# State-space stage of a hybrid decoder layer: x's transposes and the spread of a group norm's factor emitted later in the first six groups

## The chip, the cores and the metric

One core of a Trainium2 chip runs the whole kernel. The metric is the time of one execution in device microseconds (us); of several runs the median is told. Engines are named as the profile names them: PE (TensorE, matmuls), DVE (VectorE), ACT (ScalarE), POOL (GpSimd) and SP, whose queue issues the DMAs.

## The reference

One layer over 544 columns: 512 tokens of a prompt and 8 x 4 sample tokens, with 1024 channels. Cut to the part that matters here:

```
z, xbc, dt, q, k, v, qi, ki, wi, g_ssd, g_att = split(u @ w_in)
xbc = silu(causal_dwconv(xbc, buf, conv_w, conv_b))      # width 4
x, B, C = split(xbc)                  # 8 groups: 256 of x, 128 of B, 128 of C each
a_cs = cumsum(dt * a)                 # in chunks of 128 tokens
y_diag = (C @ B^T * decay) @ (x * dt)                    # inside a chunk
state  = B^T @ (x * dt * to_end)                         # from chunk to chunk
y = (y_diag + C @ state * exp(a_cs) + d_skip * x) * silu(z)
y = y * rsqrt(mean(y*y over the 256 channels of a group) + eps) * norm_g
merged = sigmoid(g_ssd) * (y @ w_br_ssd) + sigmoid(g_att) * (y_att @ w_br_att)
```

Before it lies a feed-forward network, after it the projection `w_out`, attention to a memory and a second feed-forward network. The sample tokens' attention `y_att` picks 256 keys of a paged cache by an indexer and gathers their rows. All is fp32.

## The kernel before, in words

Activations lie with channels on the 128 partitions and the 544 columns along the free axis. A product of weights is made in fp32 precision as three passes over operands that are split in a high and a low part (`mm`, line 310: wh·uh, wh·ul, wl·uh, each as 256 and 288 columns, so a product of 8 k-blocks has 48 matmuls). `weights` loads a panel by SP (L267), ACT casts its high part `wh` (L270), DVE subtracts the low part `wl` (L271). `split` does the same for an activation (L318 on ACT, L319 on DVE).

The order of the work is made by `weave` (L104 to L130) when the program is built. Each part of the work is a generator; `yield cost, delay` adds `cost` to a virtual clock and lets that generator sleep for `delay` more. The first generator in the list whose time has come goes on; the last one is the filler. So a `delay` sets how much of other generators' work is emitted before the next step of this one. The engines then run their own queues in the emitted order, and wait by semaphores for one another.

In the state-space stage (`ssd`, L1265) three generators are woven:

- the sample's attention: rounds of the indexer's top k, `sample_select`, `sample_att`. It turns the chosen slots into row addresses, gathers rows `kv` of the cache, transposes the gathered keys (pkT, L1644), makes the scores and the weights `Pm`, turns these (pPT, L1673) and copies them to PN (DVE, L1677), and multiplies by the values (pO, L1681, L1688);
- `tails`: for each of 8 groups g (0 to 7) `ssd_y(g)`: C·B (pcb, L1351; masked to cb by DVE, L1353), B's transposes (pbt, L1357), then after a delay x's transposes (pxt, L1367: four blocks of each of the group's two tiles of x, XO0 and XO1), from which DVE makes xd and xe (L1368, L1370), decay factors abc (ACT, then a product with cb on POOL or DVE, L1380), the sample's small pieces (pcs, L1384; Bs, L1401), chunk states (pst, L1413), the sample's states, y (pY, pYo), and the norm: mean of squares (st, L341), rsqrt in small steps on DVE (L345 to L331), then after a delay the factor's spread over partitions (DVE writes a diagonal zt, L352 and L354; PE spreads it, psr, L355 and L356), y times factor (L1522) and the store to `yssd_d`;
- the filler `fronts`: for each group `ssd_x(g)`, four products of 128 channels in the order B, C, XO0, XO1, each followed by copies (ACT, L1316), four convolution taps (ACT L1324, DVE L1326 three times), tanh (ACT, L1328) and a last DVE step (L1329); then `ssd_z(g)`, two products and their zt. Products of group g+2 start when y of group g is done. After the last group come the load and split of the attention's output (`att_in`, L1712) and eight products with `w_br_att` (`att_out`), times a gate `gt` (L1720).

After the stage the rows of the convolution's state are turned and stored (L1536 to L1539), and `merge` follows: it loads the 16 tiles of y (yt, L1748, three buffers), splits them into yh and yl, woven with what is left of `att_out`, and multiplies them by `w_br_ssd`.

The lines of the change are L1360 (the delay between B's and x's transposes), and L333, L348 and L1518 (the delay between the mean and the spread of the factor; line 1518 is the only caller in this stage).

Of the kernel before, what the change touches and what calls it, by code (L numbers as in the profile page):

```python
# [168 lines left out]
class Net:  # L169
# [160 lines left out]
            nc.vector.tensor_tensor(t, t, xh, op=ALU.mult)  # L330
            nc.vector.scalar_tensor_tensor(y, t, 1.5, y, op0=ALU.add, op1=ALU.mult)  # L331

    def rms(self, sqs, inv_n, pool):  # L333


        nc = self.nc
        st = self.ps1("st")
        blk = [(i * P, min(P, T - i * P)) for i in range(5)]
        for i, (c0, n) in enumerate(blk):
            for j, sq in enumerate(sqs):  # L340
                nc.tensor.matmul(st[:n, i:i + 1], sq[:, c0:c0 + n], self.ones[:, :1], start=(j == 0), stop=(j == len(sqs) - 1))  # L341
        w = pool.tile([P, 4, 5], F32, tag="nw", name="nw", bufs=2)
        x, xh, y, t = (w[:, i, :] for i in range(4))
        nc.vector.memset(x, 1.0)
        nc.vector.tensor_scalar(x[:, :4], st[:, :4], inv_n, EPS, op0=ALU.mult, op1=ALU.add)  # L345
        nc.vector.tensor_scalar(x[:32, 4:], st[:32, 4:5], inv_n, EPS, op0=ALU.mult, op1=ALU.add)
        self.rsqrt(y, x, xh, t)
        yield 0.3, 4.0  # L348

        sq = sqs[0]  # L350
        ps = self.ps1("psr")
        nc.vector.tensor_tensor(sq[:, :TP].rearrange("p (i c) -> p i c", i=4), self.ident.unsqueeze(1).broadcast_to([P, 4, P]),  # L352
                                y[:, :4].unsqueeze(2).broadcast_to([P, 4, P]), op=ALU.mult)
        nc.vector.tensor_scalar(sq[:32, TP:], self.ident[:32, :32], y[:32, 4:], None, op0=ALU.mult)  # L354
        nc.tensor.matmul(ps, self.ones, sq[:, :TP], start=True, stop=True)  # L355
        nc.tensor.matmul(st[:, 64:96], self.ones[:32, :], sq[:32, TP:], start=True, stop=True)  # L356
        yield 1.0
        return ps, st[:, 64:96]
# [979 lines left out]
    def ssd_y(self, g, z):  # L1338
        nc, I, O, sp = self.nc, self.I, self.O, self.sp
# [17 lines left out]
            nc.tensor.transpose(ps[:, c * P:(c + 1) * P], BO[:, c * P:(c + 1) * P], self.ident)  # L1357
        Bt = sp.tile([P, 4, P], F32, tag="hT_", name="Bt", bufs=2)
        nc.scalar.copy(Bt.rearrange("p a b -> p (a b)"), ps)
        yield 0.5, 2.5  # L1360
        hcol = lambda t: t.rearrange("p (c h) -> p c h", c=4)[:, :, 4 * g:4 * g + 4]
        xd = sp.tile([P, 4, 4, 64], F32, tag="xd", name="xd")
        xe = sp.tile([P, 4, 4, 64], F32, tag="xe", name="xe")
# [151 lines left out]
        nc.vector.tensor_tensor(zts[0], zts[0], zts[1], op=ALU.add)  # L1515
        sqs = zts[:1]
        yield 0.0, 9.0
        r, rs = yield from self.rms(sqs, 1.0 / 256, sp)  # L1518
        for i in range(2):
            tl = 2 * g + i  # L1520
            for o, m in ((Y[i][:, :TP], r), (Y[i][:, TP:], rs)):
# [563 lines left out]
```

## Time and profile before

| | |
|---|---|
| time, median of 3 runs | 2201.06 us (2200.52 to 2204.1) |
| the profiled execution | 2201.23 us, span 2199.4 us |
| mean granted clock of PE, profiled | 0.979 |
| PE busy in the span | 2101.4 us (96%) |
| DVE, ACT, POOL busy | 1324.2, 955.2, 444.4 us |
| state-space stage and start of the merge | about 850 to 1450 us |

The times of the trace are microseconds from the start of the span. The span is 1.8 us shorter than the execution's own time, which is 0.17 us over the median. PE is busy nearly all the time; its waits are told by a view of their own, and the granted clock (1.00 is the full one) is told for any stretch.

### The profile page before, as it was taken

The numbers are of one execution on the slowest core, as the hardware profiler recorded it, in microseconds if no ns is written. First come the engines' busy times: TensorE is split into PE (matmuls) and PEld (weight loads), VectorE is DVE, ScalarE is ACT, GpSimd is POOL, SyncE is SP. The second block draws the span as 40 slices with busy tenths as digits, with TensorE's granted clock in tenths as the row PEclk, the third lists the DMA queues.
The fourth block names the chain that finished last, engine by engine and source line by source line (L and its number), as shares of the span: only waits on it lengthen the run. The fifth ranks groups of instructions, "written<-read, shape, count | busy, mean of one in ns | idle before, by whom it ended". The sixth has DMA issues, their size and how long they took to land.

```text
span 2199.4 us, 41232 instructions
## 1 busy us (share of the span) xinstructions
PE 2101.4 (96%) x16675; PEld 1960.6 (89%) x16675; DVE 1324.2 (60%) x2711; ACT 955.2 (43%) x1821; POOL 444.4 (20%) x461
## 2 busy tenths in 40 slices
PE   7999999999999999998999999999999979999998
PEld 7999999998788678897888889999987879999998
DVE  6543334475697989896677668544563475424455
ACT  6323345345445665453556445323535443222233
POOL 0000011032122302225555641012320320000011
PEclk9999999999999999998999999999999999999999
DMA  6424565347442223355456636564443433233243
GB/s 199 126 82 128 165 203 197 113 133 213 135 127 83 88 77 110 117 157 161 126 174 192 178 106 186 175 190 155 144 149 139 154 115 115 76 96 90 81 131 100
DMA packets 320107, 301.70 MB, mean 137 GB/s; under 512 B 25416, under 2 KB 290632, under 8 KB 318868
## 3 DMA queue, kind: packets, MB, share of 16 engines
q1 hardware_dynamic: 310508, 272.58, 40.5%
q0 software_dynamic: 8448, 25.18, 3.7%
q8 instruction: 131, 2.15, 0.4%
q10 hardware_dynamic: 960, 1.31, 0.2%
q14 instruction: 60, 0.49, 0.1%
HBM read 261.14 MB, written 37.35 MB: 136 GB/s over the span
## 4 chain that ended last, share of the span: by engine, by line
PE 72%; DVE 13%; DMA 6%; ACT 4%; issue 3%; POOL 2%; SPq 0%; DVEq 0%; ACTq 0%; POOLq 0%
PE pg L310 42%; PE pgh L310 14%; PE pmo L591 2%; DVE wl L271 2%; ACT wh L270 2%; DMA wr<-in_ffn_wu 1%; DVE gtm L1077 1%; DVE XO L1326 1%; DMA yt<-yssd_d 1%; DMA abc<-ac_d 1%; PE pmkT L1811 1%; POOL sqh L370 1%; PE pmo L1878 1%; DVE XO L1329 1%; DMA wr<-in_ffn_wg 1%
## 5 line engine op out<-in xcount | busy, mean ns | idle before, releaser
L270 ACT CAST wh<-wr 128x1024 fp32r<-128x1024 f32 (+3 forms) x362 | 341.6, 959 | 512.1 <-PE pg L310 288.2
L271 DVE TENSOR_TENSOR wl<-wr,wh 128x1024 fp32r<-128x1024 f32 (+3 forms) x338 | 391.1, 1171 | 222.6 <-ACT wh L270 215.8
L310 PE MATMUL pg<-uh,wh 128*128 128x256 f32 (+1 forms) x2336 | 504.1, 297 | 0.8 <-DVE zt L1291 0.8
L310 PE MATMUL pg<-ul,wh 128*128 128x256 f32 (+1 forms) x2336 | 493.4, 292 | 0.0
L310 PE MATMUL pg<-uh,wl 128*128 128x256 f32 (+1 forms) x2336 | 491.6, 291 | 0.0
L310 PEld LDWEIGHTS pg<-uh,wh 128*128 128x128 f32 x2336 | 380.4, 191 | 21.2 <-issue 17.2
L310 PEld LDWEIGHTS pg<-ul,wh 128*128 128x128 f32 x2336 | 381.2, 191 | 2.9 <-issue 2.2
L310 PEld LDWEIGHTS pg<-uh,wl 128*128 128x128 f32 x2336 | 380.0, 190 | 1.8 <-issue 1.4
L310 PE MATMUL pgh<-uh,wh 128*128 128x288 f32 (+2 forms) x880 | 260.8, 299 | 9.5 <-ACT wh L270 6.1
L310 PE MATMUL pgh<-uh,wl 128*128 128x256 f32 (+2 forms) x880 | 260.3, 298 | 7.3 <-DVE wl L271 7.3
L310 PE MATMUL pgh<-ul,wh 128*128 128x256 f32 (+1 forms) x880 | 257.1, 294 | 0.0
L310 PEld LDWEIGHTS pgh<-uh,wh 128*128 128x128 f32 (+1 forms) x880 | 170.4, 195 | 13.2 <-ACT wh L270 7.0
L310 PEld LDWEIGHTS pgh<-uh,wl 128*128 128x128 f32 (+1 forms) x880 | 169.5, 193 | 11.1 <-DVE wl L271 10.1
L310 PEld LDWEIGHTS pgh<-ul,wh 128*128 128x128 f32 x880 | 171.4, 195 | 0.9 <-issue 0.8
L370 POOL TENSOR_TENSOR sqf<-sqf,sqt 128x256 f32<-128x256 f32 (+1 forms) x48 | 52.4, 1092 | 508.9 <-ACT sqt L369 508.6
L310 PE MATMUL pgh<-hh,wh 128*128 128x288 f32 (+1 forms) x352 | 101.9, 290 | 0.0
L310 PE MATMUL pgh<-hh,wl 128*128 128x288 f32 (+1 forms) x352 | 101.2, 288 | 0.3 <-DVE wl L271 0.3
L310 PE MATMUL pgh<-hl,wh 128*128 128x288 f32 (+1 forms) x352 | 101.4, 288 | 0.0
L1326 DVE SCALAR_TENSOR_TENSOR XO<-CB,convw,XO 128x600 f32<-128x600 f32 x96 | 86.2, 899 | 7.1 <-ACT XO L1324 6.6
L702 POOL DMA_INDIRECT G<-in_cache_kidx,ix x16 | 16.4, 1025 | 361.7 <-DVE ix L697 281.2
L617 DVE TENSOR_TENSOR g<-pg,rt 128x544 f32<-128x544 f32 x32 | 23.2, 725 | 101.1 <-PE pg L310 101.1
L620 DVE TENSOR_TENSOR g<-pg,g 128x544 f32<-128x544 f32 x32 | 23.2, 725 | 99.1 <-PE pg L310 99.1
(608 smaller groups left out, 3875.4 us busy)
## 6 DMA issues: line engine op xcount, KB each, us to landing
wr<-in_w_in SPq DMA_DIRECT2D x66, 512.0 KB
wr<-in_ffn_wg SPq DMA_DIRECT2D x48, 512.0 KB
wr<-in_ffn_wu SPq DMA_DIRECT2D x48, 512.0 KB
wr<-in_ffn_wd SPq DMA_DIRECT2D x44, 384.0 KB
wr<-in_ffn_wd SPq DMA_DIRECT2D x44, 320.0 KB
kt_d<-KT SPq DMA_DIRECT2D x8, 1024.0 KB
KT<-kt_d SPq DMA_DIRECT2D x16, 512.0 KB
wr<-in_w_in SPq DMA_DIRECT2D x32, 256.0 KB
```

The source lines that it names most:

```text
L270: nc.scalar.copy(hi[:, s], r)
L271: (lo_eng or nc.vector).tensor_tensor(lo[:, s], r, hi[:, s].bitcast(F32), op=ALU.subtract)
L310: nc.tensor.matmul(o, a[:, k, c0:c0 + m], x[:, r0:r0 + n], start=(k == 0 and j == 0), stop=(k == KT - 1 and j == 2))
L370: (nc.vector if last else nc.gpsimd).tensor_tensor(acc[:, :n], acc[:, :n], s[:, :n], op=ALU.add)
L591: nc.tensor.matmul(ps[:, :256], a[:, k, i * P:(i + 1) * P], b[:, k, :], start=(k == 0 and j == 0), stop=(k == 7 and j == 2))
L617: nc.vector.tensor_tensor(g1[:, :n], pg, rt[:, sl], op=ALU.mult)
L620: nc.vector.tensor_tensor(g1[:, :n], pu, g1[:, :n], op=ALU.mult)
L1077: nc.vector.scalar_tensor_tensor(G, S, thr[:, j:j + 1], one, op0=ALU.is_ge, op1=ALU.mult, accum_out=cnt[:, j:j + 1])
L1326: nc.vector.scalar_tensor_tensor(xo, CB[:, j:j + 600], cw(j), xo, op0=ALU.mult, op1=ALU.add)
L1329: nc.vector.scalar_tensor_tensor(xo, th, 1.0, xo, op0=ALU.add, op1=ALU.mult)
L1811: nc.tensor.transpose(ps[:, (z * 2 + i) * P:(z * 2 + i + 1) * P], mk[:, i, (k + z) * P:(k + z + 1) * P], self.ident)
L1878: nc.tensor.matmul(ps[:, d * 256:(d + 1) * 256], mv[:, x, h * 256 + d * P:h * 256 + (d + 1) * P], PT[:, x, :], start=(x == 0), stop=(x == 1))
```

## The change

Two delays get longer for groups 0 to 5. No instruction is added, taken away or altered; what is altered is the place of the steps in each engine's queue.

```diff
-    def rms(self, sqs, inv_n, pool):
+    def rms(self, sqs, inv_n, pool, late=4.0):
...
         self.rsqrt(y, x, xh, t)
-        yield 0.3, 4.0
+        yield 0.3, late
...
         nc.scalar.copy(Bt.rearrange("p a b -> p (a b)"), ps)
-        yield 0.5, 2.5
+        yield 0.5, 6.0 if g < 6 else 2.5
         hcol = lambda t: t.rearrange("p (c h) -> p c h", c=4)[:, :, 4 * g:4 * g + 4]
...
         yield 0.0, 9.0
-        r, rs = yield from self.rms(sqs, 1.0 / 256, sp)
+        r, rs = yield from self.rms(sqs, 1.0 / 256, sp, 7.0 if g < 6 else 4.0)
```

Since all three generators share one clock, everything behind such a delay is dealt out anew. Three places show it. The number behind a name is that of its buffer or tile; "x4" are four instructions in a row.

**Place 1, PE in group 2**, from the last matmul of XO1's product to the sample's small pieces. Before:

```order
L310 MATMUL pg_10648<-uh_75,wl_10563 128x288
...
L1351 MATMUL pcb_10760<-XO3_10553,XO2_10467 128x128 x4
L1357 MATMUL pbt_10769<-ident_69,XO2_10467 128x128 x4
...
L1367 MATMUL pxt_10806<-ident_69,XO0_10638 128x128 x4
...
L1367 MATMUL pxt_10813<-ident_69,XO1_10722 128x128 x4
L1384 MATMUL pcs_10842<-ident_69,XS_10356 96x128 x3
```

and now:

```order
L310 MATMUL pg_10616<-uh_75,wl_10480 128x288
...
L1351 MATMUL pcb_10848<-XO3_10470,XO2_10371 128x128 x4
L1357 MATMUL pbt_10859<-ident_69,XO2_10371 128x128 x4
...
L1577 MATMUL pslot_10904<-ct_7276,row_10715 128x32 x2
...
L1634 MATMUL psS_10945<-mk_5255,lt_10946 128x256
L1635 MATMUL psS_10945<-bn_5256,En_10943 128x32
L1367 MATMUL pxt_10973<-ident_69,XO0_10606 128x128 x4
L1367 MATMUL pxt_10980<-ident_69,XO1_10670 128x128 x4
L1384 MATMUL pcs_11007<-ident_69,XS_10277 96x128 x3
```

From the first row to the transposes of XO1 there were 67 matmuls in the queue and there are 159 now; in groups 0 to 7 there were 71, 126, 67, 83, 64, 84, 77, 64, and there are 85, 181, 159, 91, 145, 181, 173, 159. The address step of the gathered rows (pslot) and the start of the sample's scores now stand ahead of them. From pslot to the first transposes of gathered keys (L1644) there were 63 matmuls, and there are 92.

**Place 2, DVE in the norm of group 2**, from the mean to the two writes of the diagonal that psr waits for (`nw` holds the factor). Before:

```order
L345 TENSOR_SCALAR nw_11448<-st_11442 128x4
L346 TENSOR_SCALAR nw_11448<-st_11442 32x1
L1326 SCALAR_TENSOR_TENSOR XO2_11412<-CB0_8947,convw_558,XO2_11412 128x600
...
L1669 TENSOR_SCALAR Pm_11487<-Pm_11487,sv_11488 128x288
...
L1628 COPY qz_10969<-qs_5257 64x16 x2
...
L1329 SCALAR_TENSOR_TENSOR XO2_11412<-th_11417,XO2_11412 128x600
...
L352 TENSOR_TENSOR zt0_10884<-ident_69,nw_11448 128x512
L354 TENSOR_SCALAR zt0_10884<-ident_69,nw_11448 32x32
```

and now:

```order
L345 TENSOR_SCALAR nw_11598<-st_11592 128x4
L1326 SCALAR_TENSOR_TENSOR XO0_11562<-CB0_8947,convw_558,XO0_11562 128x600
L346 TENSOR_SCALAR nw_11598<-st_11592 32x1
...
L326 TENSOR_SCALAR nw_11598<-nw_11598 128x5
...
L1329 SCALAR_TENSOR_TENSOR XO0_11562<-th_11567,XO0_11562 128x600
L352 TENSOR_TENSOR zt0_10785<-ident_69,nw_11598 128x512
L354 TENSOR_SCALAR zt0_10785<-ident_69,nw_11598 32x32
```

The sample attention's small steps (L1628, L1669) no longer lie in between. On PE there were 54 matmuls from the mean (st) to psr in this group, and there are 71; in groups 0 to 7 there were 123, 77, 54, 51, 43, 45, 62, 41, and there are 137, 78, 71, 77, 71, 47, 29, 41. Of group 6's, 57 were matmuls of line 310 before and 24 are now; of group 7's 36 both times.

**Place 3, ACT at the start of the merge**: the last row of the convolution's state (nco), casts of weight panels (wh) and of y tiles (yh). Before:

```order
L1536 COPY nco_15648<-pnc_15655 27x512
L270 CAST wh_15995<-wr_15997 128x1024
L270 CAST wh_15995<-wr_16001 128x1024
L318 CAST yh0_15901<-yt_15899 128x544
...
L318 CAST yh4_15925<-yt_15923 128x544
L270 CAST wh_16108<-wr_16110 128x1024
```

and now:

```order
L1536 COPY nco_15788<-pnc_15795 27x512
L270 CAST wh_16108<-wr_16110 128x1024
L270 CAST wh_16108<-wr_16114 128x1024
L318 CAST yh0_15901<-yt_15899 128x544
...
L318 CAST yh4_15925<-yt_15923 128x544
```

`wh_16108` takes the buffer of the panel that the last product of `att_out` reads. On PE, 192 matmuls of line 310 stood between group 7's psr and the merge's first product; 84 stand there now, so `att_out` is further on when the stage ends.

## Rows read from the trace of the kernel before

**Rows 1.** The page of the profile, its first part: busy time, share of the span and instructions of each engine, in one line.
```profile
PE 2101.4 (96%) x16675; PEld 1960.6 (89%) x16675; DVE 1324.2 (60%) x2711; ACT 955.2 (43%) x1821; POOL 444.4 (20%) x461
```

**Rows 2.** The waits of TensorE (PE) in the stretch 850 to 1450 us, which holds the state-space stage and the start of the merge: what waited, for what, then microseconds in total, times, and the longest.
```profile
PE pxt L1367 <- DVE XO L1329: 10.4, 3, 5.3
PE psr L355 <- DVE zt L352: 7.0, 3, 3.7
PE pO L1681 <- DVE PN L1677: 3.7, 1, 3.7
PE pkT L1644 <- DMA kv<-in_cache_k,slot: 2.2, 2, 1.4
PE ph L1438 <- DVE H L1420: 0.9, 1, 0.9
PE pst L1413 <- DVE xe L1370: 0.9, 1, 0.9
PE pg L310 <- DVE yl L319: 0.8, 1, 0.8
PE pg L310 <- DVE zt L1291: 0.8, 1, 0.8
PE pg L310 <- ACT yh L318: 0.6, 2, 0.4
PE pst L1413 <- DVE Bs L1401: 0.6, 1, 0.6
```

**Rows 3.** The timeline of PE, x's transposes of groups 0, 2 and 5 (start, duration, engine, line, operation, shapes, and in brackets the idle time before it with its releaser).
```profile
862.08 0.66 PE L1367 MATMUL pxt<-ident,XO 128*128 128x128 f32 x4 [1.06 <-DVE XO L1329]
...
994.67 1.11 PE L1367 MATMUL pxt<-ident,XO 128*128 128x128 f32 x4 [5.34 <-DVE XO L1329]
...
1218.75 0.65 PE L1367 MATMUL pxt<-ident,XO 128*128 128x128 f32 x4 [4.03 <-DVE XO L1329]
```

**Rows 4.** Six stretches of the state-space stage, which are all the time between 850 and 1450 us in which the granted clock stands at 0.50: length, busy time with its instructions of PE, PEld, DVE, ACT and POOL, granted clock, DMA share, GB/s.
```profile
922.99:929.82 6.83, 5.59 (x18) 4.02 (x19) 4.95 (x10) 0.05 (x1) 0.13 (x1) 0.50 0.21 82
991.25:998.08 6.83, 3.41 (x15) 2.96 (x16) 6.82 (x13) 1.50 (x3) 0.27 (x1) 0.50 0.00 1
1018.56:1025.39 6.83, 5.98 (x28) 5.55 (x28) 2.24 (x8) 0.58 (x1) 5.42 (x8) 0.50 0.54 153
1059.52:1062.93 3.41, 3.41 (x17) 3.28 (x16) 2.55 (x6) 0.25 (x1) 0.00 (x0) 0.50 0.63 173
1219.95:1223.36 3.41, 3.41 (x22) 2.72 (x20) 2.82 (x10) 0.00 (x0) 2.52 (x3) 0.50 0.35 94
1284.80:1291.63 6.83, 5.78 (x38) 5.07 (x39) 3.91 (x7) 1.50 (x3) 3.46 (x5) 0.50 0.12 35
```

**Rows 5.** One undisturbed stretch in the same columns, of the matmuls of line 310 alone (PE and PEld busy, granted clock, DMA share, GB/s).
```profile
1406.00:1412.00 6.00, 6.00 (x50) 6.00 (x49) 1.00 0.19 56
```

**Rows 6.** The timeline of PE, the spread of the norm's factor (psr) in groups 0, 2 and 4.
```profile
924.23 2.08 PE L355 MATMUL psr<-zt,ones 128*128 128x512 f32 x2 [3.74 <-DVE zt L352]
...
1058.23 1.12 PE L355 MATMUL psr<-zt,ones 128*128 128x512 f32 x2 [2.73 <-DVE zt L352]
...
1201.59 1.09 PE L355 MATMUL psr<-zt,ones 128*128 128x512 f32 x2 [0.51 <-DVE zt L352]
```

**Rows 7.** The timeline of DVE, POOL and PE around two of these norms: group 0 from the mean to the last row before psr, and the bare chain of group 7 with its psr.
```profile
906.89 0.16 DVE L345 TENSOR_SCALAR nw<-st 128x4 f32<-128x4 f32 x1
...
912.09 5.35 POOL L271 TENSOR_TENSOR wl<-wr,wh 128x1024 fp32r<-128x1024 f32 x2 [3.77 <-ACT wh L270]
...
912.72 2.39 DVE L331 SCALAR_TENSOR_TENSOR nw<-nw 128x5 f32<-128x5 f32 x1
...
1388.22 0.16 DVE L345 TENSOR_SCALAR nw<-st 128x4 f32<-128x4 f32 x1 [1.72 <-PE st L341]
...
1392.72 1.02 PE L355 MATMUL psr<-zt,ones 128*128 128x512 f32 x2
```

**Rows 8.** The timeline of POOL and DVE at three places where a product of POOL (L1380) lies beside a DVE row, and one row of L1329 with nothing beside it.
```profile
974.66 0.79 DVE L1329 SCALAR_TENSOR_TENSOR XO<-th,XO 128x600 f32<-128x600 f32 x1 [0.69 <-ACT th L1328]
...
1213.38 4.66 POOL L1380 TENSOR_TENSOR abc<-abc,cb 128x1024 f32<-128x1024 f32 x2
...
1213.43 5.26 DVE L1329 SCALAR_TENSOR_TENSOR XO<-th,XO 128x600 f32<-128x600 f32 x1
...
1278.73 6.14 POOL L1380 TENSOR_TENSOR abc<-abc,cb 128x1024 f32<-128x1024 f32 x2 [0.92 <-DVE cb L1353]
...
1285.43 0.27 DVE L1677 COPY PN<-pPT 32x128 f32<-32x128 f32 x1
```

**Rows 9.** The timeline at the start of the merge: the last output row of the convolution's state and the first loads of y on SP's queue (SPq), the first and the last split of a y tile on ACT and DVE.
```profile
1404.10 0.30 SPq L1539 DMA_DIRECT2D out_nconv_s<-nco  x1
...
1411.69 1.27 SPq L1748 DMA_DIRECT2D yt<-yssd_d  x3
...
1415.79 1.32 ACT L318 CAST yh<-yt 128x544 fp32r<-128x544 f32 x2 [4.09 <-DMA yt<-yssd_d]
...
1416.47 0.73 DVE L319 TENSOR_TENSOR yl<-yt,yh 128x544 fp32r<-128x544 f32 x1 [3.33 <-ACT yh L318]
...
1440.45 1.60 DVE L319 TENSOR_TENSOR yl<-yt,yh 128x544 fp32r<-128x544 f32 x2 [1.54 <-ACT yh L318]
```

**Rows 10.** The timeline of DVE at the start of the attention's output, the last three rows of its split.
```profile
1361.63 2.00 DVE L319 TENSOR_TENSOR ul<-yat,uh 128x544 fp32r<-128x544 f32 x3
```

## Prediction, written before the changed kernel was run

> **What bounds the kernel now.** First the page [rows 1]: PE is busy for 96% of the span, so a gain can only come from PE's waits or from its clock. Then PE's waits in the stretch that the change reorders [rows 2]: x's transposes wait three times for the last DVE step of x's tile (10.4 us), the spread of the norm's factor three times for its diagonal (7.0 us), and the sample's attention once for PN and twice for gathered keys (3.7 and 2.2 us). All the rest is under 1 us each. Then the granted clock: between 850 and 1450 us it stands at 0.50, the lower of the two levels (1.2 GHz), in six stretches [rows 4], and each opens in or right behind a wait: four of them where a transpose of x or a spread waited [rows 3, 6], the one at 1018 us with the gathered keys, the one at 1284 us with PN, whose copy starts at 1285.43 [rows 8]. Matmuls of line 310 follow one another at 6.00 us / 50 = 0.12 us at the full level [rows 5]; at half of it the same work takes twice as long, so a half-clock stretch costs half of its PE busy time: 2.8, 1.7, 3.0, 1.7, 1.7 and 2.9 us in the order of [rows 4].
>
> **The change part by part.** The same instructions run, so the working is about waits alone. The sum is made against the profiled execution (2201.23 us), 0.17 us above the median shown.
>
> *A, x's transposes.* They wait 1.06, 5.34 and 4.03 us in groups 0, 2 and 5 [rows 3], because the last DVE step of XO1 has not run. Place 1 shows at least 14 matmuls more between XO1's product and these transposes in group 0 (71 to 85), 92 more in group 2 and 97 in group 5. At 0.12 us these are 1.7, 11 and 11.6 us, each over the wait. All 10.4 us go, and the half-clock stretches at 991 and 1220 us with them (1.7 + 1.7): **13.8**.
>
> *B, the norm's spread.* In group 2 it waits 2.73 us [rows 6] and gets 17 matmuls more and a DVE queue without the sample's steps (place 2): the wait goes, and the stretch at 1060 us (1.7). Group 4 loses its 0.51 us. In group 0 it waits 3.74 us; there DVE's rsqrt runs from 906.89 to past 915 because one step took 2.39 us beside a POOL subtraction [rows 7]. The 14 matmuls it gains are 1.7 us, and two DVE subtractions of weights now stand in the chain too, about as long; I keep this wait and its clock. **4.9**.
>
> *C, gathered keys.* From the addresses (pslot) to the first key transposes lie 29 matmuls more, 3.5 us, against 2.2 us of waiting [rows 2]; with the stretch at 1018 us (3.0): **5.2**.
>
> *D, PN.* The DVE copy to PN is a 0.27 us row that starts at 1285.43, when the two POOL products that began at 1278.73 and took 6.14 us have just ended [rows 8]. In the new order every turn of the sample's weights stands ahead of the next group's pcb, without which POOL cannot start its product. Wait (3.7) and stretch (2.9) go: **6.6**.
>
> *E, chunk states.* pst waits 0.9 and 0.6 us [rows 2]; between x's transposes and pst there now lie 27 to 40 matmuls instead of 19 to 35: **1.5**.
>
> Gains: 13.8 + 4.9 + 5.2 + 6.6 + 1.5 = 32.0.
>
> *F, the start of the merge.* What the filler no longer does late, it has done early: between group 7's psr and the merge's first product 108 matmuls of line 310 fewer hide the loads of y. Before, psr at 1392.72 [rows 7], first yl at 1416.47, last done at 1442.05 [rows 9], 15 tiles in 25 us; PE waits 0.8 + 0.6 us there [rows 2], so it had no slack to speak of. If the loads come as late as now, PE loses 108 x 0.12 = 13 us, 14.4 with the waits that it has: the upper bound. They can come earlier, since SP's loads stood behind a gate load that waited, from 1404.10 to 1411.69 [rows 9]; if they start 7.6 us earlier and nothing else holds them, 13.0 - 7.6 = 5.4. But place 3 puts yh0 behind two casts that need att_out's last product to end, at 84 x 0.12 + the small pieces, some 15 us behind psr; with two casts and a split the first yl is at about +19 instead of +24, and the last ends 25 us later as now, 5 us earlier than before. By that it is 13.0 - 5 = 8. I take a value between the two: **6.5**, a half-clock stretch in it, with the bounds 0 (the loads catch up) and 14.4.
>
> *G, psr of groups 1, 6 and 7.* Bare, the chain from the mean to psr takes 4.5 us (1388.22 to 1392.72) [rows 7]; 24 matmuls of line 310 in group 6 are 2.9 us, with a few small ones beside. **1.2**, between 0 and 3.
>
> *H, from the last state-space product to att_out.* Group 7's z is followed by att_out's first product after 10 matmuls, 17 before; the split of its operand ends in a 2.00 us DVE row group at 1363.63 [rows 10]. **2**, between 0 and 5.
>
> *Queues.* The moved steps take their DMAs along: the loads of Es behind pst and the stores of states and of y on SP. abc's loads stand ahead of the delay and do not move against it. PE shows no wait for a weight's load in this stretch [rows 2], so SP's other order is priced at nothing; without the three buffers of panels that cover it, the price would be the time of such a load, and it would show as a wait for wh.
>
> *I, new collisions.* Each product on POOL is shifted against DVE. **3**, half of what one such meeting cost (wait 4.0 and clock 1.7 in group 5), between 0 and 8.
>
> Costs 12.7; net -19.3; 2201.2 - 19.3 = 2181.9, say **2182 us**.
>
> **A rule weighed against a row.** L1329 takes 0.79 us with nothing beside it, and 5.26 us where it starts 0.05 us after POOL's product (1213.43 and 1213.38) [rows 8]. The Trainium skill, page "SBUF — State Buffer", section "Who interferes with whom", says why: a DVE instruction with two SBUF inputs and a GpSimd instruction that reads SBUF take turns on one shared port pair, and the later one blocks fully. The trace agrees with that in this row. By that rule a product that is emitted later takes its lock along and meets another DVE row: the time would be that of rival 1 below, 2194, where the sum above has 2182.
>
> **The rivals.**
>
> *1, the meetings move.* abc's product and L1329 or PN meet elsewhere: for it speaks that a dozen POOL products of line 1380 (two a group, but one in groups 1 to 4, by the code) share the stage with the 128 rows of L1326 and L1329 (four for each of 32 tiles); against it that only three of eight groups show a wait now. Priced as C and D given back elsewhere (11.8): 2201.2 - 19.3 + 11.8 = **2194**.
>
> *2, the wait moves down its own chain.* pst or the y products wait for xd and xe where pxt waited for x: A and E (15.3) come back, and half of the 11.8 of C and D. For it: pst does wait for xe now, 0.9 us [rows 2]. Against it: 27 and more matmuls follow x's transposes. 2201.2 - 19.3 + 15.3 + 5 = **2202**, no change.
>
> *3, more than I count.* Group 0's spread is covered too (3.7 + 2.8), the merge's loads catch up to within 1 us, and nothing collides (3): another 15 us, **2167**.
>
> *4, slower: the merge's loads lie bare.* They come as late behind psr as now, because the casts and the gates keep SP's and ACT's queues in order, and PE loses 14.4 us there. With G, H and I (6.2) that is 20.6; it decides when B, C and D give less than 5.3 of their 16.7, since A and E bring 15.3. With none of them: 2201.2 - 15.3 + 20.6 = **2206**. For it: PE has no slack in the merge today [rows 2]; against it: the gate load that delays SP's queue ends earlier when att_out is further on.
>
> That the change does nothing is excluded: places 1 to 3 show other queues.
>
> **How the numbers follow.** A measurement of this kernel can tell 0.2%, 4.4 us, from no change. Forecast 0.45, rival 1 0.25, rival 2 0.12, rival 3 0.10, rival 4 0.08. Faster: the forecast but for a little, most of rival 1, and rival 3, 0.75; same: rival 2 and the rest of those, 0.16; slower: rival 4 and a little of rival 2, 0.09. The range goes from rival 3 (2166, a little under its 2167) to the edge of rival 2 (2200); beyond it lie rival 4 and about half of rival 2 and, below, a tenth of rival 3's.
>
> **What would show it.** In the changed kernel's profile: no wait of pxt for XO, and PE's half-clock stretches in this stage two or three instead of six (A, C, D); psr of group 2 without a wait and of group 0 with about 3.7 us (B); pO without a wait for PN (D); waits for yh and yl at the merge of about 7 us together instead of 1.4 (F). If pst or pY wait for xd or xe, rival 2 holds; if new rows of 3 us and more stand beside POOL's products with a PE wait behind them, rival 1; if the merge waits over 14 us, rival 4. The forecast is wrong if the sum of PE's waits and half-clock losses between 850 and 1450 us falls by less than 10 us.

## The result, and the profile after

The changed kernel takes **2186.1 us** (median of 4 runs, 2184.32 to 2188.54) where the kernel before takes 2200.89 (four runs, among them the three told ahead of the prediction): a ratio of 0.993 (95% interval 0.9913 to 0.9948), 14.8 us less. On a second occasion it was 2185.25 us and 0.993 (0.9913 to 0.9946). The forecast was 2182, with a range of 2166 to 2200: the direction was right, the size 4 us too large, and several of its terms were far from what the runs showed.

First the waits of PE in the same stretch, 850 to 1450 us, of the changed kernel (compare [rows 2]; columns as there).

```profile
PE psr L355 <- DVE zt L352: 7.3, 3, 4.1
PE pg L310 <- ACT yh L318: 4.2, 2, 2.4
PE pst L1413 <- DVE Bs L1401: 3.2, 3, 1.6
PE pg L310 <- DVE wl L271: 1.7, 1, 1.7
PE pst L1413 <- DVE od L1692: 1.5, 3, 0.7
PE pst L1413 <- DVE cbs L1390: 1.2, 1, 1.2
PE pO L1681 <- DVE PN L1677: 1.2, 2, 0.6
PE pg L310 <- DVE yl L319: 1.1, 2, 0.9
```

The waits of x's transposes (10.4 us) and of gathered keys (2.2) are gone and PN's is down from 3.7 to 1.2. In their place pst waits 6.2 us where it waited 1.5, and the merge (yh, wl, yl) 7.0 where it waited 1.4. The spread of the norm's factor waits as long as before, though elsewhere, as will be seen.

Then the stretches at half clock, all of them between 850 and 1450 us (compare [rows 4]; same columns).

```profile
989.55:996.38 6.83, 6.83 (x23) 5.26 (x24) 4.21 (x9) 0.59 (x1) 1.38 (x1) 0.50 0.31 101
1078.30:1081.71 3.41, 3.41 (x16) 3.32 (x15) 1.27 (x3) 1.73 (x6) 2.26 (x3) 0.50 0.51 145
1402.57:1409.40 6.83, 6.07 (x27) 6.07 (x28) 3.39 (x6) 1.80 (x4) 0.00 (x0) 0.50 0.75 213
1436.70:1440.11 3.41, 3.41 (x17) 3.41 (x17) 3.41 (x4) 0.92 (x2) 1.71 (x1) 0.50 0.65 188
```

Four instead of six, each behind one of the new waits; two of them lie in the merge, where there was none. By half of PE's busy time they cost 9.9 us, 13.8 before (9.8 and 14.0 by the count of the table below).

Third, x's transposes of group 5 and the DVE step that they need, in the timeline of the changed kernel (compare [rows 3, 8]).

```profile
1197.58 0.78 DVE L1329 SCALAR_TENSOR_TENSOR XO<-th,XO 128x600 f32<-128x600 f32 x1
...
1211.73 1.03 PE L1367 MATMUL pxt<-ident,XO 128*128 128x128 f32 x8
```

The step takes 0.78 us instead of 5.26 and is done 13 us before PE comes to it. No row of L1329 in the changed kernel takes over 0.79 us. Before, XO1's transposes started within 0.5 us of that step's end in four of eight groups.

Summed over the stage, from B's first transposes to the merge's last matmul: the third column is its length, the fourth PE's idle time in it, the fifth half of PE's other time at half clock, the sixth what is left of the length. The times come from four occasions, on which the kernel before took 2200.9 to 2203.5 us; each ratio is taken within its occasion.

| kernel | us (ratio to before) | stage | idle | half clock | rest |
|---|---|---|---|---|---|
| before | 2200.89 | 666.7 | 29.6 | 14.0 | 623.1 |
| changed | 2186.1 (0.993) | 653.5 | 24.3 | 9.8 | 619.4 |
| x's delay alone | 2182.25 (0.9903) | 648.6 | 19.0 | 6.1 | 623.5 |
| the same again | 2185.24 (0.9931) | 650.4 | 17.8 | 8.9 | 623.8 |
| norm's delay alone | 2193.05 (0.9957) | 655.6 | 21.6 | 11.3 | 622.8 |
| changed, gate panels on DVE | 2173.78 (0.986) | 642.9 | 18.1 | 6.4 | 618.5 |
| changed, six y buffers | 2176.43 (0.9888) | 642.2 | 19.7 | 5.0 | 617.5 |
| changed, both | 2168.43 (0.986) | 633.4 | 13.5 | 1.5 | 618.4 |

### The profile page after: what moved, and what is told of

Read it like the earlier page. It is cut to its first block, busy times and chain, and to the rows that moved or that the text cites. A ratio compares the mean times of both kernels' runs of the same rounds, so it can differ in the third digit from the quotient of the medians.

```text
span 2186.8 us, 41207 instructions
## 1 busy us (share of the span) xinstructions
PE 2093.5 (96%) x16675; PEld 1958.1 (90%) x16675; DVE 1322.9 (60%) x2711; ACT 956.8 (44%) x1821; POOL 443.5 (20%) x461
## 4 chain that ended last, share of the span: by engine, by line
PE 73%; DVE 13%; ACT 5%; DMA 4%; issue 3%; POOL 2%; SPq 0%; DVEq 0%; ACTq 0%; POOLq 0%
PE pg L310 42%; PE pgh L310 16%; PE pmo L591 2%; DVE wl L271 2%; ACT wh L270 2%; DVE gtm L1077 1%; DMA wr<-in_ffn_wu 1%; DMA yt<-yssd_d 1%; DVE XO L1326 1%; PE ph L1438 1%; PE pmkT L1811 1%; POOL sqh L370 1%; PE pmo L1878 1%; ACT Pm L1196 1%; DVE Pm L1202 1%
## 5 line engine op out<-in xcount | busy, mean ns | idle before, releaser
L271 DVE TENSOR_TENSOR wl<-wr,wh 128x1024 fp32r<-128x1024 f32 (+3 forms) x338 | 395.1, 1182 | 220.6 <-ACT wh L270 216.8
L310 PE MATMUL pg<-ul,wh 128*128 128x256 f32 (+1 forms) x2336 | 487.1, 289 | 0.0
L310 PEld LDWEIGHTS pgh<-uh,wl 128*128 128x128 f32 (+1 forms) x880 | 169.8, 194 | 10.6 <-DVE wl L271 9.0
```

The source lines that it names most:

```text
L271: (lo_eng or nc.vector).tensor_tensor(lo[:, s], r, hi[:, s].bitcast(F32), op=ALU.subtract)
L310: nc.tensor.matmul(o, a[:, k, c0:c0 + m], x[:, r0:r0 + n], start=(k == 0 and j == 0), stop=(k == KT - 1 and j == 2))
```

## The experiments

**One delay at a time.** First x's alone:

```diff
-        r, rs = yield from self.rms(sqs, 1.0 / 256, sp, 7.0 if g < 6 else 4.0)
+        r, rs = yield from self.rms(sqs, 1.0 / 256, sp, 4.0)
```

> The change's delay of x's transposes alone (6.0 in groups 0 to 5); the norm's delay is back at 4.0. In this order x's transposes stand 85, 87 and 96 matmuls behind XO1's product in groups 0, 2 and 5 (71, 67, 84 before; 85, 159, 181 with both delays), the norm's spread of group 2 stands 43 behind its mean (54 before), and 160 matmuls of line 310 are left between group 7's psr and the merge (192 before, 84 with both). My theory (a wait goes by as many matmuls as are put ahead of it, 0.12 us each): pxt still waits 5.3 - 2.4 = 2.9 us in group 2 and 4.0 - 1.4 = 2.6 in group 5, the spread of group 2 waits 4 us instead of 2.7; 2194 to 2199 us. Rival (the delay of x is all that counts): the gain of both, 2184 to 2188 us.

Measured: 2182.25 us, ratio 0.9903 (0.9885 to 0.9921), 12 us under the least that was expected. No transposes of x wait, though groups 2 and 5 got only 20 and 12 matmuls more, which at 0.12 us each are 2.4 and 1.4 us against waits of 5.3 and 4.0. So in this kernel the matmuls put ahead are not enough to explain why the waits went. What remains, in the waits of PE from 850 to 1450 us, is the norm,

```profile
PE psr L355 <- DVE zt L352: 9.0, 3, 4.3
```

in groups 0, 1 and 2 (3.0, 4.3 and 1.7 us). Then the norm's alone:

```diff
-        yield 0.5, 6.0 if g < 6 else 2.5
+        yield 0.5, 2.5
```

> The change's delay of the norm's spread alone (7.0 in groups 0 to 5); x's delay is back at 2.5. In this order x's transposes stand 71, 65 and 74 matmuls behind XO1's product in groups 0, 2 and 5, the spread 80, 71 and 68 behind the mean in groups 2, 3 and 4 (54, 51, 43 before), and the merge's cover is 192 matmuls as before. My theory: no wait of psr in groups 2 and 4, the three waits of pxt (10.4 us) stay or move by a microsecond, no wait more at the merge; about 5 us less than before, 2193 to 2198 us. Rival (the norm's delay is of no use alone): 2199 to 2202 us.

Measured: 2193.05 us, 0.9957 (0.9941 to 0.9973): 9.5 us less by the ratio, where about 5 were expected. The waits of PE in the same stretch:

```profile
PE pxt L1367 <- DVE XO L1329: 5.3, 2, 4.3
PE psr L355 <- DVE zt L352: 4.3, 2, 3.7
...
PE pO L1681 <- DVE PN L1677: 1.1, 1, 1.1
```

Group 5's wait for x and most of PN's went too, though x's transposes are as close behind x's product as before (74 matmuls, 84 before). Again it is not cover: the DVE step of group 5 now runs at 1204.67 us and takes 0.78, and the product on POOL that it met before starts at 1208.90.

Since x alone looked better than both, the two ran once more side by side:

> The changed kernel once more, beside the one with x's delay alone, so that the two stand on one chip. Theory from the traces so far: in the changed kernel the norm's delay costs on top of x's delay, about 5 us in this stage (653.5 against 648.6 us from the first transposes of B to the merge's last matmul), by waits of chunk states and by less cover at the merge: 2184 to 2188 us, 3 to 6 more than with x's delay alone. Rival (the difference of the two is chance of the profile): within 2 us of it.

> The delay of x's transposes alone, once more, on the same chip as the changed kernel. Theory: 3 to 6 us less than the changed kernel, 2180 to 2183 us. Rival: the same as it.

Measured: 2185.25 and 2185.24 us. The theory that the norm's delay costs 3 to 6 us fell. It is worth about 9 us alone and nothing measurable on top of x's: in these two profiles it removes the spread's wait in group 2 (2.3 us) and shortens the rest by 4.9, and gives somewhat more back at pst (1.4 to 4.7) and the merge (2.5 to 7.9).

**What x's transposes waited for.** The product of the decay factors on POOL was left out of the kernel before in groups 5 and 6:

```diff
-            (nc.vector if 1 <= g <= 4 and i else nc.gpsimd).tensor_tensor(abc[i], abc[i], cb.rearrange("p c t -> p (c t)").unsqueeze(1).broadcast_to([P, 2, TP]), op=ALU.mult)
+            g not in (5, 6) and (nc.vector if 1 <= g <= 4 and i else nc.gpsimd).tensor_tensor(abc[i], abc[i], cb.rearrange("p c t -> p (c t)").unsqueeze(1).broadcast_to([P, 2, TP]), op=ALU.mult)
```

> The kernel before, without the product of the decay factors with C.B in groups 5 and 6 (four instructions on POOL; y of these two groups is not the reference's). It tests whether POOL's products cause the wait of x's transposes in group 5 (4.03 us) and of PN in group 6 (3.70 us). Theory: L1329 at 1213 us takes 0.8 us instead of 5.3, both waits go with their half-clock stretches (1.7 and 2.9): about 12 us less, 2187 to 2191 us. Rival (the DVE rows are late for another reason, their own queue or ACT): the waits stay, 2199 to 2202 us.

Measured: 2192.92 us, 0.9957 (0.994 to 0.9973). In the timeline of DVE and PE, group 5:

```profile
1211.04 0.79 DVE L1329 SCALAR_TENSOR_TENSOR XO<-th,XO 128x600 f32<-128x600 f32 x1
...
1212.17 0.60 PE L1367 MATMUL pxt<-ident,XO 128*128 128x128 f32 x4
```

Both waits are gone, with no matmul put ahead of anything and nothing else altered. The stage is 12.3 us shorter, as expected; the time fell by 9.5 us by its ratio and lies 2 us above the expected range. So group 5's wait in the kernel before was its own group's product on POOL holding the DVE step that x's transposes need. PN's wait in group 6 went with the product too.

Two more runs tried to part the product's place from the cover, by emitting the decay factors' work (L1374 to L1380) behind the sample's small pieces in the kernel before, and ahead of the delay in the changed kernel.

> The kernel before with PE's order unchanged, in which only the decay factors' work (relu, exp and product with C.B, L1374 to L1380) is emitted later, behind the sample's small pieces and their delay instead of ahead of them. It asks whether x's transposes can be freed without a matmul more ahead of them. Theory now (the waits of pxt in group 5 and of PN in group 6 come from the group's own product on POOL, which holds the DVE rows that they need): both waits go, group 2's falls from 5.3 to 3 us or less; 2188 to 2194 us. Rival (only cover on PE helps, as the prediction had it): the waits stay, 2199 to 2202 us.

> The changed kernel with the decay factors' work emitted ahead of the longer delay of x's transposes, so that POOL's product starts as early against x's convolution as before the change while x's transposes keep their cover of 85 to 181 matmuls. Prediction's step A (the matmuls put ahead cover the wait): DVE rows of x of 3 to 5 us beside POOL's product come back, but pxt does not wait over 1 us; 2183 to 2188 us. Rival (the change helps by moving the product away from x's last DVE step, and the cover is idle): waits of pxt of 3 us and more in group 2 or 5, 2190 to 2196 us.

Measured: 2201.68 us (1.0, 0.999 to 1.0011) and 2187.36 us (0.994, 0.9927 to 0.9952). Neither decides: in the first one the product kept its place in POOL's queue, and the timeline shows the old picture.

```profile
1210.44 5.27 DVE L1329 SCALAR_TENSOR_TENSOR XO<-th,XO 128x600 f32<-128x600 f32 x1
...
1210.40 4.66 POOL L1404 TENSOR_TENSOR abc<-abc,cb 128x1024 f32<-128x1024 f32 x2
...
1215.77 1.12 PE L1367 MATMUL pxt<-ident,XO 128*128 128x128 f32 x4 [4.04 <-DVE XO L1329]
```

In the second one no DVE step of x's tiles met the product either, so its cover was not put to the test. What sets the product's place differs by group. In groups 0, 1, 6 and 7 of the kernel before POOL waits for its other operand, C.B (pcb, masked to cb). In group 5 cb was done at 1209.29 us, and the product stood behind four gathers of values in POOL's queue (timeline of POOL in the kernel before):

```profile
1212.42 0.95 POOL L1618 DMA_INDIRECT kv<-in_cache_v,slot  x1 [0.30 <-issue]
1213.38 4.66 POOL L1380 TENSOR_TENSOR abc<-abc,cb 128x1024 f32<-128x1024 f32 x2
```

In the queue of PE, pcb stood 13 to 16 matmuls behind the end of XO1's product in six of eight groups of the kernel before, and in the changed kernel 83 to 164 in six of eight. The delays make the tail of most groups fall behind the filler.

**The new wait of the spread in group 1.** The gate panels' low parts of columns 2 and 3 go to DVE, in the changed kernel:

```diff
-            w = self.win((C_GS, C_GA)[x] + c * 256, lo_eng=self.nc.gpsimd)
+            w = self.win((C_GS, C_GA)[x] + c * 256, lo_eng=None if x and c in (2, 3) else self.nc.gpsimd)
```

> The changed kernel, with the low parts of the gate panels of columns 2 and 3 subtracted by DVE instead of POOL (two panels, four subtractions). It is a test of the new wait of psr in group 1 (4.06 us, with a half-clock stretch of 6.83 us at 989 us): in it two small DVE rows take 2.35 us each beside POOL's subtraction (4.80 us, 976.12 to 980.92). Theory (DVE rows are held up by POOL's): those rows fall to about 0.3 us, two DVE subtractions of 1.2 us come into the queue; the wait falls to 2.5 us or less, group 0's falls too; 2181 to 2185 us. Rival (the chain is long by what stands in it, and POOL does no harm): the wait grows by 2.4 us; 2188 to 2190 us.

Measured: 2173.78 us, 0.986 (0.9841 to 0.9879), more than the theory had asked for. The place in the changed kernel, from POOL's, DVE's and PE's timelines, group 1:

```profile
976.12 4.80 POOL L271 TENSOR_TENSOR wl<-wr,wh 128x1024 fp32r<-128x1024 f32 x2 [0.57 <-ACT wh L270]
...
976.33 2.35 DVE L1566 TENSOR_SCALAR dum<-pgf,ptf 128x256 f32<-128x256 f32 x1
...
978.60 2.35 DVE L326 TENSOR_SCALAR nw<-nw 128x5 int32<-128x5 int32 x1
...
989.55 2.07 PE L355 MATMUL psr<-zt,ones 128*128 128x512 f32 x2 [4.06 <-DVE zt L352]
```

The second step of rsqrt, on 5 columns, takes 2.35 us. With the edit it takes 0.15 (timeline of DVE), and all the spreads together wait 0.8 us instead of 7.3 (waits of PE):

```profile
968.91 0.15 DVE L326 TENSOR_SCALAR nw<-nw 128x5 int32<-128x5 int32 x1
```

```profile
PE psr L355 <- DVE zt L352: 0.8, 2, 0.5
```

**The merge.** Six buffers for the tiles of y instead of three, in the changed kernel:

```diff
-                yt = ep.tile([P, T], F32, tag="yt", name="yt", bufs=3)
+                yt = ep.tile([P, T], F32, tag="yt", name="yt", bufs=6)
```

> The changed kernel with six buffers for the tiles of y at the merge instead of three. All 16 loads of y now stand ahead of the 2.2 MB load of the residual (L1765), which in the changed kernel stands ahead of the last four. Theory (the last loads of y are late because that load is ahead of them): the wait of 1.8 us for the thirteenth tile at 1427 us goes, and a half-clock stretch behind it; the first wait (2.4 and 0.9 us, yh0 behind two casts on ACT) stays; 2 to 4 us less than the changed kernel, 2181 to 2184 us. Rival (the loads of y are late by their number alone): no difference. A second one: panels of w_br_ssd now stand behind the y tiles and their casts come late, a wait for wl or wh of 2 us and more in its place.

Measured: 2176.43 us, 0.9888 (0.987 to 0.9906), 8.8 us less than the changed kernel beside it, where 2 to 4 were expected. The merge of the changed kernel, from the timelines of ACT, PE and SP's queue:

```profile
1399.20 1.99 ACT L270 CAST wh<-wr 128x1024 fp32r<-128x1024 f32 x2 [4.16 <-PE pg L310]
1401.10 1.73 ACT L318 CAST yh<-yt 128x544 fp32r<-128x544 f32 x3
...
1401.79 0.64 PE L310 MATMUL pg<-yh,wh 128*128 128x256 f32 x3 [2.38 <-ACT yh L318]
...
1416.14 0.43 SPq L1765 DMA_DIRECT2D hT<-h_d  x1
...
1426.75 1.94 ACT L318 CAST yh<-yt 128x544 fp32r<-128x544 f32 x3 [6.96 <-DMA yt<-yssd_d]
...
1427.44 0.76 PE L310 MATMUL pg<-yh,wh 128*128 128x256 f32 x4 [1.83 <-ACT yh L318]
```

PE is held up twice by tiles of y: first yh0 stands behind two casts that wait for PE itself (4.16 us), then a later tile comes late, because the residual's load (2.2 MB) was issued ahead of it. The Trainium skill, page "DMA: Bandwidth & Descriptors", section "Queues, rings and completion order", says that each DMA engine takes a ring's descriptors in order; the trace agrees, with 7 us in which ACT waits for a tile of y behind that load. With six buffers only the first of the two is left (timeline of PE), and half-clock time falls from 8.2 to 5.0 us (against the run beside it); the wait for wl at 1436 us is gone too. Of the 8.8 us, the waits at the merge are 4.6 (7.9 to 3.3) and half-clock time there 1.5; the rest lies elsewhere in the stage, and it is not shown that the edit brought it. The edit moves the residual's load behind the tiles and adds buffers at once, which is not parted either.

```profile
1393.75 0.63 PE L310 MATMUL pg<-yh,wh 128*128 128x256 f32 x3 [2.38 <-ACT yh L318]
1395.29 0.64 PE L310 MATMUL pg<-yl,wh 128*128 128x256 f32 x2 [0.91 <-DVE yl L319]
```

**Together.** The two mends on x's delay alone, and on the changed kernel:

> The delay of x's transposes alone, with the gate panels' low parts on DVE and six buffers of y: the version that the runs so far point to. Against x's delay alone: group 0's and group 1's spread (3.0 and 4.3 us, half-clock stretches of 3.41 and 6.83 us) go, as they did in the changed kernel with the same edit (12 us less there), and the late y tiles (2.6 us, a stretch of 3.41): 2181 - 11 - 3 = 2167 us, between 2163 and 2172. Rival (the gains overlap, since a later wait takes over what an earlier one gives up): 2172 to 2178 us.

> The changed kernel with both mends, the gate panels' low parts on DVE and six buffers of y. If the two are independent (ratios of 0.986 and 0.989 against the changed kernel's 0.993): 0.982 of before, 2160 to 2166 us. If they overlap: 2168 to 2174 us.

Measured: 2173.12 us, 0.9874 (0.9854 to 0.9895), and **2168.43 us**, 0.986 (0.9844 to 0.9875), the lowest time of all. Both come out at the overlapping end: the stage shrinks by 20.1 us, nearly the 10.6 and 11.3 of the two mends added, but the ratio of the times is that of the gate panels alone. Which of the two tells more is not settled by these runs.

**A delay more.** On that kernel, the chunk states later as well:

```diff
-        yield 0.5, 2.5
+        yield 0.5, 4.5 if g < 7 else 2.5
         CZ = sp.tile([P, 288], F32, tag="CZ", name="CZ")
```

> The changed kernel with both mends (gate panels on DVE, six buffers of y), and the delay ahead of the chunk states (pst) 4.5 instead of 2.5 in groups 0 to 6. In this order 40 to 50 matmuls stand between the sample's small pieces and pst instead of 17 to 33, but only 52 matmuls of line 310 are left between group 7's psr and the merge instead of 84. Theory (what the tail gets later, the filler has done earlier, and the merge pays): pst's waits (7.2 us in five groups) fall under 2 us, and the first waits at the merge grow from 3.3 us by up to 32 x 0.12 = 3.8 us; 2164 to 2168 us, at most a little under the version without it (2168 us). Rival (the waits of pst are free to take): 2159 to 2163 us.

Measured: 2172.29 us, 0.986 (0.9835 to 0.9884): no gain. pst's waits fell from 7.2 to 0.6 us. The merge took 3.7 of that back (timeline of PE), and the wait for gathered values, 0.3 us in the kernel without this delay, 3.8 (waits of PE):

```profile
1393.03 1.03 PE L310 MATMUL pg<-yh,wh 128*128 128x256 f32 x3 [6.53 <-ACT yh L318]
```

```profile
PE pO L1688 <- DMA kv<-in_cache_v,slot: 4.1, 4, 1.7
```

At the merge 3.3 us had become 7.0 (6.5 + 0.5): the 32 matmuls of cover that it lost are 3.8. All idle time of the stage together grew by 1.1 us only; what made this profile's stage longer is mostly half-clock time, 7.4 us instead of 1.5, and only 2.3 of the 7.4 lie in the merge. The profiled run is the slowest of its four here and was the fastest of its four there, so this difference is at the high end.

## Why the prediction was right or wrong, step by step

- **A, x's transposes (-13.8):** the effect was right, 10.4 us of waiting and the two half-clock stretches are gone. The reason was right in part at most. The step said that matmuls put ahead cover the wait, and took the length of the DVE rows as given. With x's delay alone the matmuls would have covered half of it, and all of it went. In the changed kernel x's last DVE step ends 16 and 14 us ahead of XO1's transposes in groups 2 and 5, so there the cover could have done it too; that was not parted. In group 5 the product on POOL made the wait, shown by leaving it out. In group 2 L1329 of XO1 itself took 0.77 us, and three DVE rows ahead of it ran beside POOL's work, in the timelines of the kernel before:

```profile
982.00 2.47 POOL L271 TENSOR_TENSOR wl<-wr,wh 128x1024 fp32r<-128x1024 f32 x1
982.75 2.37 DVE L1329 SCALAR_TENSOR_TENSOR XO<-th,XO 128x600 f32<-128x600 f32 x1 [0.51 <-ACT th L1328]
985.48 2.39 POOL L271 TENSOR_TENSOR wl<-wr,wh 128x1024 fp32r<-128x1024 f32 x1
985.97 2.04 DVE L1566 TENSOR_SCALAR dum<-pgf,ptf 128x256 f32<-128x256 f32 x1
987.83 2.42 POOL L1380 TENSOR_TENSOR abc<-abc,cb 128x1024 f32<-128x1024 f32 x1
987.94 2.95 DVE L1326 SCALAR_TENSOR_TENSOR XO<-CB,convw,XO 128x600 f32<-128x600 f32 x1
```

Rows of these lines take 0.79, 0.35 and 0.83 us elsewhere; the three lost 5.4 us together, as much as the wait (5.34). No run took these meetings alone away, so for group 2 this is argued from the rows.

- **B, the spread (-4.9):** groups 2 and 4 lost their waits and group 0 kept 3.0 of 3.7, as said. But with x's delay in place this part is worth nothing in the end.
- **C and D (-5.2, -6.6):** the waits for gathered keys went, as said; PN's wait fell by 2.5 of 3.7. Both half-clock stretches behind them are gone.
- **E, chunk states (-1.5): wrong in sign.** pst waits 4.7 us more. The few matmuls more between x's transposes and pst were not enough, because a DVE row on the way to the sample's small pieces, for which pst waits, now meets the product that was moved. It is another row in each of the three groups that hold 5.9 of the 6.2 us: L1397 in group 3, a subtraction of weights in group 5, L1391 in group 6 (0.27, 1.2 and 0.27 us elsewhere). No run left the product out of the changed kernel, so this is argued from the rows of POOL's, DVE's and PE's timelines:

```profile
1073.47 2.96 DVE L1397 CAST xes<-xef 96x256 fp32r<-96x256 f32 x1
1073.91 2.36 POOL L1380 TENSOR_TENSOR abc<-abc,cb 128x1024 f32<-128x1024 f32 x1
...
1207.69 6.12 DVE L271 TENSOR_TENSOR wl<-wr,wh 128x1024 fp32r<-128x1024 f32 x1 [2.12 <-ACT wh L270]
1207.97 4.75 POOL L1380 TENSOR_TENSOR abc<-abc,cb 128x1024 f32<-128x1024 f32 x2
...
1279.65 4.74 POOL L1380 TENSOR_TENSOR abc<-abc,cb 128x1024 f32<-128x1024 f32 x2
...
1281.72 2.82 DVE L1391 TENSOR_TENSOR Gs<-dec_s,cbs 32x128 f32<-32x128 f32 x1
...
1285.73 0.67 PE L1413 MATMUL pst<-xe,Bt 128*128 128x256 f32 x2 [1.10 <-DVE Bs L1401]
```

- **F, the merge (+6.5): mis-sized.** The waits come to the 7 us forecast, 5.6 more than before, though 1.7 of them are for wl, which the sum did not name; the half-clock time that follows them is 4.7, where 6.5 leaves about 1. The first wait is the one described. The second came from a load that the sum had not looked at: the residual's, which had stood behind all y tiles.
- **G, the spread of the other groups (+1.2): mis-sized.** The price counted PE's matmuls; group 1 had as many as before (78 for 77) and waits 4.06 us, with a half-clock stretch of 3.4 (half of 6.83) behind it. What had changed was DVE's chain, which now runs beside POOL's subtraction. The spreads of groups 6 and 7 do not wait.
- **H and I:** no wait at the start of att_out (0, not 2). The new collisions are those in E and G.

The rival that came true in part is the first: meetings of DVE with POOL moved, to L1391, L1397, L271 and L326, and cost up to 4.7 (pst) and 7.5 us (the spread of group 1), near the 11.8 that it priced, only that C and D did not come back with them. (Rival 2's sum took 5 for half of 11.8, which is 5.9; that changes nothing.)

Idle and half-clock time in the stage together changed by -9.5 us, where the prediction had -19.3. By its own sign, a fall of less than 10 us between 850 and 1450 us, the forecast stands on the edge: it is about 9 us in this profile and about 10 in the second one of the same kernel. There are also four half-clock stretches (five in the second profile), not two or three. So it is in part luck that the time came within 4 us of the forecast. The profiled stage is 13.2 us shorter; the 3.7 left over lie in the column "rest", which is 617 to 619 us in all kernels with both delays and 623 to 625 in those with one or none. The number of changes between line 310 and small matmuls (285 before, 277 in the changed kernel) does not follow it across the kernels, and its cause stays open. Half-clock time also differs between two profiles of the same kernel (9.8 and 8.2 us for the changed one), so single stretches are not to be read too closely.

## What to carry to other kernels

Before a wait is priced by how many matmuls could cover it, look at the duration of the row that it waits for, and of the rows ahead of that one: a step of 5.26 us that took 0.79 elsewhere was held up by another engine here, and it was free again when the other one's work was left out or lay elsewhere. A delay in a woven order moves all that follows, so ask which pairs of engines will newly run side by side, and what the end of the stage loses when the filler has been used up early. Two delays that cure the same lag need not add: here they did not.

## What the runs showed of the hardware

A DVE instruction on 5 columns with one input, 0.15 us by itself, took 2.35 us beside a subtraction of POOL (two such rows fill the 4.80 us of POOL's two subtractions); a two-input one on 600 columns took 5.26 us beside two products of 4.66 us in all. The Trainium skill, page "SBUF — State Buffer", section "Who interferes with whom", lists `tensor_scalar` among the operations that can take the ports shared with POOL when their operands meet its conditions, as well as those with two SBUF inputs; both rows agree. Not expected was its price here: four subtractions moved from POOL to DVE made the kernel some 12 us faster, 10.6 of them in this stage, though DVE had 4 x 1.2 us more to do.
